# Tree attention: a pair's matmuls grouped by array form, GpSimd's queue written out, V copied by fours

## The chip, the core and the metric

The kernel runs on one core of a Trainium2 chip. The core has a matmul engine (PE, TensorE), whose weights are loaded by separate instructions (PEld); VectorE (DVE); ScalarE (ACT); GpSimd (POOL), which also issues most of the DMAs here; and SyncE (SP), which only issues DMAs. PE writes to PSUM, from which DVE and ACT read; the other tiles are in SBUF. The metric is the device time of one execution in microseconds (us), lower is better.

## The reference

Q, K and V are 8 x 12 x 512 x 64 in fp32: 96 heads of 512 positions. Position i may attend to itself and to its ancestors in a binary heap (parent of i is (i-1)//2), and to nothing else.

```python
scores = np.einsum('bhqd,bhkd->bhqk', Q, K) * scale      # scale = 1/sqrt(64)
scores = scores + (1 - mask) * (-1e9)
weights = np.exp(scores - np.max(scores, axis=-1, keepdims=True))
weights = weights / (np.sum(weights, axis=-1, keepdims=True) + 1e-10)
return np.einsum('bhqk,bhkd->bhqd', weights, V).astype(np.float32)
```

## The kernel before

The heads are worked in **pairs** (pair i is heads 2i and 2i+1, 48 pairs), loaded and stored in **groups** of four (group q is pairs 2q and 2q+1, 24 groups), and the values V lie in buffers of eight heads, called **octets** here (octet o is pairs 4o to 4o+3, 12 octets). A query needs few keys: the top levels of the tree, which all share (one tile of 128 keys, "e1"), and a second tile of 128 keys that depends on the query's quarter ("e2").

A pair takes these steps:

- `transpose(i)` (L227): 32 small PE transposes bring K and Q into the order of the tree, in PSUM (`kqp`); `evac(i)` (L253) copies them to SBUF (`kq`) on DVE.
- `scores1(i)` (L264, L269) and `scores2(i)` (L286, L295): PE writes the mask as a product of codes and adds K·Q; ACT takes the exponential of each (L275, L300) into `e1` and `e2`.
- `values(i, a)` for each head a of the pair (L316, L321, L327): e1 and e2 times V, into `ob`. V has a column of ones, so the sum of the weights comes out beside the values.
- `norm(i)` (L339, L340): DVE takes the reciprocal of that sum and multiplies, into `of`. When both pairs of a group are done, `store` (L348) writes 512 KB.

The tiles that are handed from PE to ACT and DVE (`s1`, `s2`, `kqp`, `ob`) have one buffer each, two PSUM banks of the eight: the values of pair i cannot begin before `norm(i-1)` has read `ob`, and so on.

V comes in by position and must be brought into the order of the tree before it is used as the right operand `vt` (three buffers, one octet each). That is done by copies between partitions: `spread_top` (L193, four copies on POOL for an octet), `spread_l7` (L213, four copies on DVE) and `spread_leaves` (L201, two on DVE). Some copies have a half form of four heads (`h0`, `h1`).

PE uses the array in three forms in this kernel. In the page's rows they are 128\*64 (transposes and the 64-column products of L327), 64\*128 (the scores) and 128\*128 (L316, L321).

The order on every engine is the order of the program text (`manual_schedule`). POOL's queue holds loads, V copies and stores in one line, and an instruction that waits holds back all behind it. So does DVE's queue. Before the main loop, groups 0 to 3 are loaded, pairs 0 and 1 transposed, and octet 0 of V copied by fours. In iteration i: `scores1(i)`, `values(i-1, 0)`, `scores2(i)`, `values(i-1, 1)`, `norm(i-1)`, `transpose(i+2)`, `evac(i+2)`, then V copies of octet i//4+1, then a group of loads (six groups ahead) and, at odd i, a store (six groups back).

Of the kernel before, what the change touches and what calls it, by code (L numbers as in the profile page):

```python
# [26 lines left out]
SELF = (2, 3, 2, 3)  # L27
# [69 lines left out]
def kernel(  # L97
# [54 lines left out]
    NV = 3  # L152
# [11 lines left out]
    qsts, ksts, vsts = {}, {}, {}  # L164
    qTs, kTs, kqps, obs, ets, ofs = {}, {}, {}, {}, {}, {}

    def load_one(name, kept, src, q, parts=1):
        st = loads.tile([P, 4, 4, D], bf16, name=name)
        n = 4 // parts
        for j in range(parts):  # L170
            nc.gpsimd.dma_start(  # L171
                out=st[:, n * j:n * j + n, :, :].rearrange("p h t d -> p h (t d)"),
                in_=src[:, 4 * q + n * j:4 * q + n * j + n, :],
            )
        kept[q] = st

    def load_v(q):
        o, half = divmod(q, 2)
        if half == 0:
            vsts[o] = vloads.tile([P, 8, 4, D], bf16, name="vst")  # L180
        nc.gpsimd.dma_start(  # L181
            out=vsts[o][:, 4 * half:4 * half + 4, :, :].rearrange("p h t d -> p h (t d)"),
            in_=Vr[:, 4 * q:4 * q + 4, :],
        )

    def load(q, parts=1):
        load_one("kst", ksts, Kr, q, parts)
        load_one("qst", qsts, Qr, q, parts)
        load_v(q)

    def spread_top(o, h0=0, h1=8):
        for j in range(4):
            nc.gpsimd.tensor_copy(  # L193
                out=vts[o % NV][32 * j:32 * j + 32, h0:h1, 0, 0:D],
                in_=vsts[o][0:32, h0:h1, UNITS[TOP + j][1], :],
            )

    def spread_leaves(o, r, h0=0, h1=8):

        p = 64 if r else 0  # L200
        nc.vector.tensor_copy(  # L201
            out=vts[o % NV][p:p + 64, h0:h1, 1 + r:4 + r:2, 0:D],
            in_=vsts[o][64:128, h0:h1, r:3 + r:2, :],
        )

    def spread_l7(o, quad, h0=0, h1=8):

        first, slot, step = ((2, 0, 3), (2, 2, -1), (1, 3, -3), (1, 1, 1))[quad]
        src = vsts[o][32:64, h0:h1, slot, :]
        src = bass.AP(  # L210
            src.tensor, src.offset, [list(src.ap[0]), list(src.ap[1]), [step * D, 2], [1, D]]
        )
        nc.vector.tensor_copy(  # L213
            out=vts[o % NV][32 * quad:32 * quad + 32, h0:h1, first:first + 3:2, 0:D], in_=src
        )
# [27 lines left out]

    def evac(i):
        kq = work.tile([P, 2, 16, 32], bf16, name="kq")
        kTs[i] = kq[:, 0, :, :]
        qTs[i] = kq[:, 1, :, :].rearrange("p (t u) c -> p t (u c)", t=4)
        src = kqps[i][:, :, 0:18, :]
        src = bass.AP(
            src.tensor, src.offset,  # L250
            [list(src.ap[0]), [1024, 2], [32, 8], [9 * 32, 2], [1, 32]],
        )
        nc.vector.tensor_copy(  # L253
            out=kq[:, :, :, :].rearrange("p k (x y) c -> p k x y c", y=2), in_=src
        )
# [47 lines left out]
            func=AF.Exp, scale=scale,  # L303
        )

    def values(i, a):
        hh = 2 * (i % 4) + a
        if a == 0:
            obs[i] = psO.tile([P, 2, 512], fp32, name="ob")
        ob, e1, e2, vt = obs[i], ets[i], e2s[i % NE], vts[(i // 4) % NV]  # L310

        def o(t, lo=0, hi=128):
            return ob[lo:hi, a, 65 * t:65 * t + 65]

        for t in range(4):
            nc.tensor.matmul(  # L316
                out=o(t), lhsT=e1[:, a, t, :], rhs=vt[:, hh, 0, 0:D + 1],
                start=t == 0, stop=False,
            )
        for t in (2, 3):  # L320
            nc.tensor.matmul(  # L321
                out=o(t), lhsT=e2[:, a, t, :], rhs=vt[:, hh, 1 + t, 0:D + 1],
                start=False, stop=False,
            )
        for t in (0, 1):
            for lo, tile2 in ((0, SELF[t]), (64, t)):
                nc.tensor.matmul(  # L327
                    out=o(t, lo, lo + 64), lhsT=e2[:, a, t, lo:lo + 64],
                    rhs=vt[:, hh, 1 + tile2, 0:D + 1],
                    start=False, stop=t == 1,  # L330
                )

    def norm(i):
        q, r = divmod(i, 2)
# [15 lines left out]
            in_=ofs[q][:, h0:h0 + n, :, :].rearrange("p h t d -> p h (t d)"),  # L350
        )

    AHEAD = 6
    BEHIND = 6

    load(0, 2)
    load(1)
    spread_top(0, 0, 4)
    load(2)
    spread_top(0, 4, 8)  # L360
    load(3)
    for i in range(2):
        transpose(i)
        evac(i)
    for h in (0, 4):
        for r in range(2):
            spread_leaves(0, r, h, h + 4)
        for j in range(4):
            spread_l7(0, j, h, h + 4)

    loaded, stored = 4, 0
    for i in range(NP + 1):
        q, r = divmod(i, 2)
        if i < NP:
            scores1(i)
        if 1 <= i <= NP:
            values(i - 1, 0)
        if i < NP:
            scores2(i)
        if 1 <= i <= NP:  # L380
            values(i - 1, 1)
            norm(i - 1)
        if i + 2 < NP:
            transpose(i + 2)
            evac(i + 2)
        o = i // 4 + 1
        if o < NQ // 2:
            if i % 4 == 0:
                spread_top(o)
            if i % 4 < 2:  # L390
                spread_l7(o, 2 * (i % 4))
                spread_l7(o, 2 * (i % 4) + 1)
            else:
                spread_leaves(o, i % 4 - 2)
        if loaded < min(NQ, q + 1 + AHEAD):
            load(loaded)
            loaded += 1
        behind = BEHIND if loaded < NQ else 0
        if stored < NQ - 1 and 2 * (stored + behind) + 3 <= i and (r == 1 or loaded == NQ):
            store(nc.gpsimd, stored)  # L400
            stored += 1
        if i == NP - 1:
            store(nc.sync, NQ - 1, 0, 2)
    assert loaded == NQ and stored == NQ - 1
    store(nc.sync, NQ - 1, 2, 1)
    store(nc.scalar, NQ - 1, 3, 1)

# [29 lines left out]
```

## Time and profile before

| | |
|---|---|
| median of 11 runs | 160.11 us (159.2 to 161.58) |
| the profiled execution | 160.66 us, of it span 158.8 us |
| PE busy | 124.5 us (78%) |
| DVE busy | 113.2 us (71%) |
| POOL busy | 104.4 us (66%) |
| ACT busy | 89.0 us (56%) |
| data moved by DMA | 32.30 MB, counted at the destination |

The span is the time from the first to the last instruction on the core; the execution's time is 1.86 us longer. Loads read fp32 from HBM and write bf16 to SBUF (256 KB for a group's K, Q or V), so that the DMA bytes of a load are half of what is read. Engine shares are averages: the first 40 us look different from the rest.

### The profile page before, as it was taken

Reading aid. Unit: us, or ns where it says so; the run is one execution under the profiler, and the core shown is the slowest. Engines: PE = TensorE matmul, PEld = TensorE weight load, DVE = VectorE, ACT = ScalarE, POOL = GpSimd, SP = SyncE. Lnnn points to the kernel's source line nnn. Section 1 sums busy time; section 2 is a strip of 40 time slices with the busy share of each in tenths; the row PEclk is TensorE's granted clock in tenths of the full one; section 3 lists DMA queues with packets and bytes.
Section 4 is the critical chain, followed back from the end, with each engine's and each line's share of the span. In section 5 each row is a group of like instructions: output and inputs, shape, how many; then the busy total and the mean of one; then the engine's idle time right before and its main releaser. Section 6 shows DMA issues by size and latency. Waiting matters only on the chain.

```text
span 158.8 us, 5887 instructions
## 1 busy us (share of the span) xinstructions
PE 124.5 (78%) x2592; PEld 81.3 (51%) x2592; DVE 113.2 (71%) x229; ACT 89.0 (56%) x98; POOL 104.4 (66%) x153
## 2 busy tenths in 40 slices
PE   0386202997499999899999898999999989799860
PEld 0253101674365656575656665666667556565540
DVE  1066307653969989979889889798898997887521
ACT  3025200476156767666776767667768666577730
POOL 7848507993979799987968849769769780111010
PEclk9999855599879999999999999999999999999995
DMA  5999990899999999999999999999999999512342
GB/s 137 158 164 162 171 119 1 110 187 196 196 197 196 197 197 196 197 251 222 258 266 251 223 258 265 253 221 256 268 241 235 376 397 371 203 46 90 136 168 98
DMA packets 42090, 32.30 MB, mean 203 GB/s; under 512 B 1616, under 2 KB 38992, under 8 KB 42064
## 3 DMA queue, kind: packets, MB, share of 16 engines
q0 software_dynamic: 41360, 30.94, 109.4%
q1 hardware_dynamic: 560, 0.85, 1.6%
q8 instruction: 20, 0.33, 0.8%
q10 hardware_dynamic: 144, 0.13, 0.3%
q14 instruction: 6, 0.05, 0.1%
HBM read 38.21 MB, written 12.58 MB: 320 GB/s over the span
## 4 chain that ended last, share of the span: by engine, by line
PE 49%; DVE 21%; DMA 14%; POOL 9%; issue 4%; POOLq 0%; DVEq 0%
DMA vst<-in_V_dram 14%; PE ob L316 11%; PE ob L327 8%; DVE of L340 8%; PE kqp L227 8%; DVE vt L213 7%; PE s L286 6%; PE s L264 5%; PE s L295 4%; PE s L269 4%; DVE kq L253 3%; POOL kst L171 3%; POOL vt L193 3%; POOL qst L171 3%; PE ob L321 3%
## 5 line engine op out<-in xcount | busy, mean ns | idle before, releaser
L275 ACT ACTIVATE e<-s 128x1024 bf16<-128x1024 f32 x48 | 49.1, 1023 | 45.1 <-PE s L269 45.1
L300 ACT ACTIVATE e<-s 128x768 bf16<-128x768 f32 x48 | 38.9, 810 | 18.1 <-PE s L295 16.4
L316 PE MATMUL ob<-vt,e 128*128 128x65 bf16 x384 | 28.8, 198 | 18.7 <-DVE of L340 16.3
L193 POOL COPY vt<-vst 32x512 bf16<-32x512 bf16 (+1 forms) x52 | 32.0, 616 | 17.3 <-DMA vst<-in_V_dram 13.8
L316 PEld LDWEIGHTS <-e 128*128 128x128 bf16 x384 | 17.4, 99 | 44.6 <-DVE of L340 31.8
L253 DVE COPY kq<-kqp 128x1024 bf16<-128x1024 bf16 x48 | 32.7, 681 | 7.6 <-PE kqp L227 7.6
L213 DVE COPY vt<-vst 32x1024 bf16<-32x1024 bf16 (+1 forms) x52 | 27.2, 523 | 10.9 <-DMA vst<-in_V_dram 9.9
L340 DVE TENSOR_TENSOR of<-ob,rec 128x512 f32<-128x512 f32 x48 | 33.2, 691 | 1.7
L348 POOL DMA_DIRECT2D out_dram<-of x23 | 17.7, 769 | 22.8 <-DVE of L340 18.4
L227 PE MATMUL kqp<-ctile,kst 128*64 128x128 bf16 x384 | 20.1, 229 | 8.8 <-DMA kst<-in_K_dram 5.1
L327 PE MATMUL ob<-vt,e 128*64 128x65 bf16 x384 | 24.6, 209 | 0.0
L339 DVE RECIPROCAL rec<-ob 128x8 f32<-128x8 f32 x48 | 10.0, 208 | 19.0 <-PE ob L327 18.2
L321 PE MATMUL ob<-vt,e 128*128 128x65 bf16 x192 | 21.9, 196 | 0.0
L227 PE MATMUL kqp<-ctile,qst 128*64 128x128 bf16 x384 | 20.0, 227 | 2.3 <-DMA qst<-in_Q_dram 2.2
L171 POOL DMA_DIRECT2D qst<-in_Q_dram x25 | 19.1, 763 | 3.4 <-PE s L269 2.2
L171 POOL DMA_DIRECT2D kst<-in_K_dram x25 | 19.2, 766 | 2.1 <-POOLq L421 0.8
L181 POOL DMA_DIRECT2D vst<-in_V_dram x24 | 18.4, 768 | 1.8 <-DMA vst<-in_V_dram 1.3
L264 PE MATMUL s<-ctile 64*128 64x512 bf16 x96 | 19.4, 400 | 0.0
L269 PE MATMUL s<-kq 64*128 64x512 bf16 x96 | 19.0, 392 | 0.0
L295 PEld LDWEIGHTS <-kq 64*128 64x128 bf16 x576 | 16.7, 96 | 4.0 <-issue 1.1
L227 PEld LDWEIGHTS <-kst 128*64 128x64 bf16 x384 | 13.5, 116 | 9.3 <-DMA kst<-in_K_dram 5.4
L295 PE MATMUL s<-kq 64*128 64x64 bf16 (+2 forms) x576 | 18.0, 192 | 0.2 <-issue 0.2
(17 smaller groups left out, 87.0 us busy)
## 6 DMA issues: line engine op xcount, KB each, us to landing
out_dram<-of POOLq DMA_DIRECT2D x23, 512.0 KB, 9.5
vst<-in_V_dram POOLq DMA_DIRECT2D x24, 256.0 KB, 9.3
kst<-in_K_dram POOLq DMA_DIRECT2D x23, 256.0 KB, 8.3
qst<-in_Q_dram POOLq DMA_DIRECT2D x23, 256.0 KB, 8.9
ctile<-tree_consts SPq DMA_DIRECT2D x1, 448.0 KB, 2.9
kst<-in_K_dram POOLq DMA_DIRECT2D x2, 128.0 KB, 3.8
qst<-in_Q_dram POOLq DMA_DIRECT2D x2, 128.0 KB, 4.4
out_dram<-of SPq DMA_DIRECT2D x1, 256.0 KB, 2.2
```

Source lines behind the costliest of these rows:

```text
L171: nc.gpsimd.dma_start(out=st[:, n * j:n * j + n, :, :].rearrange("p h t d -> p h (t d)"), in_=src[:, 4 * q + n * j:4 * q + n * j + n, :],)
L193: nc.gpsimd.tensor_copy(out=vts[o % NV][32 * j:32 * j + 32, h0:h1, 0, 0:D], in_=vsts[o][0:32, h0:h1, UNITS[TOP + j][1], :],)
L213: nc.vector.tensor_copy(out=vts[o % NV][32 * quad:32 * quad + 32, h0:h1, first:first + 3:2, 0:D], in_=src)
L227: nc.tensor.transpose(out=dst, in_=st[i // 2][:, 2 * (i % 2) + a, t, :], identity=perm)
L253: nc.vector.tensor_copy(out=kq[:, :, :, :].rearrange("p k (x y) c -> p k x y c", y=2), in_=src)
L264: nc.tensor.matmul(out=sp[:, a, :], lhsT=k1code[64 * a:64 * a + 64, :], rhs=q1code[64 * a:64 * a + 64, :], start=True, stop=False,)
L275: nc.scalar.activation(out=et[:, :, :, :].rearrange("p a t c -> p (a t c)"), in_=sp[:, :, :].rearrange("p a c -> p (a c)"), func=AF.Exp, s ...
L295: nc.tensor.matmul(out=sp[:, a, t, lo:hi], lhsT=keys(i, a, TILE2[tile2]), rhs=qTs[i][64 * a:64 * a + 64, t, lo:hi], start=False, stop=(t, ...
L300: nc.scalar.activation(out=e2s[i % NE][:, :, :, 32:128].rearrange("p a t c -> p (a t) c"), in_=sp[:, :, :, 32:128].rearrange("p a t c -> p ...
L316: nc.tensor.matmul(out=o(t), lhsT=e1[:, a, t, :], rhs=vt[:, hh, 0, 0:D + 1], start=t == 0, stop=False,)
L327: nc.tensor.matmul(out=o(t, lo, lo + 64), lhsT=e2[:, a, t, lo:lo + 64], rhs=vt[:, hh, 1 + tile2, 0:D + 1], start=False, stop=t == 1,)
L340: nc.vector.tensor_tensor(out=ofs[q][:, 2 * r:2 * r + 2, :, :], in0=o4[:, :, :, 0:D], in1=rec[:, :, :, :].to_broadcast([P, 2, 4, D]), op=A ...
```

## The change

Five things change; the arithmetic, the tiles and their shapes stay, but for the number of `of` buffers.

1. **PE.** In iteration i the order is now `scores1(i)`, `scores2(i)`, then all values of pair i-1: for both heads the 128-column products, then for both heads the 64-column products (`values(i)`, one call for the pair).
2. **POOL's queue** is a generator, `pool_program`, that is advanced step by step. Group 0 comes in as K, Q of two heads, V, K, Q of the other two. From group 2 on, K and Q of group q are issued ahead of the top copies, and V behind them; the top copies belong to group q-2 (first four octets, half an octet at a time) or to octet (q-3)//2 (later).
3. **Stores** go out 12 groups behind the loads, in place of 6; `of` has 15 buffers for 9.
4. **V by fours.** For the first four octets (`FOURS = 4`) the copies on POOL and DVE are made for four heads at a time; before, octet 0 alone.
5. **DVE's V copies** stand elsewhere: half octet f (heads 4f to 4f+3, pairs 2f and 2f+1) in iterations 2f-1 and 2f, three copies in each; later octets o in iterations 4o-3, 4o-2, 4o-1, two copies in each, none in 4o. Before, octet o had two copies in each of 4o-4 and 4o-3 and one in each of 4o-2 and 4o-1.

```diff
-    opool = ctx.enter_context(tc.tile_pool(name="opool", bufs=9))
+    opool = ctx.enter_context(tc.tile_pool(name="opool", bufs=15))
...
+    def values(i):
+
+        obs[i] = ob = psO.tile([P, 2, 512], fp32, name="ob")
+        e1, e2, vt = ets[i], e2s[i % NE], vts[(i // 4) % NV]
...
+        for a in range(2):
+            for t in range(4):
+                product(e1, a, t, 0, start=t == 0, stop=False)
+            for t in (2, 3):
+                product(e2, a, t, 1 + t, start=False, stop=False)
+        for a in range(2):
+            for t in (0, 1):
+                product(e2, a, t, 1 + SELF[t], 0, 64, start=False, stop=t == 1)
+                product(e2, a, t, 1 + t, 64, 128, start=False, stop=t == 1)
...
+    def pool_program():
+
+        load_qk(0, 2)
+        load_qk(1, 1)
+        load_v(1)
+        yield
+        for q in range(2, NQ):
+            load_qk(q, 1)
+            if q < 2 * FOURS + 2:
+                o, half = divmod(q - 2, 2)
+                spread_top(o, 4 * half, 4 * half + 4)
+            elif q % 2 == 1:
+                spread_top((q - 3) // 2)
+            load_v(q)
+            yield
+            if q >= BEHIND:
+                store(nc.gpsimd, q - BEHIND)
+        spread_top(NQ // 2 - 1)
+        for q in range(NQ - BEHIND, NQ - 1):
+            yield
+            store(nc.gpsimd, q)
+
+    def spread_vector(i):
+
+        for f in range(2 * FOURS):
+            o, h = divmod(f, 2)
+            if f == 0 and i == 0:
+                parts = range(6)
+            elif f > 0 and i in (2 * f - 1, 2 * f):
+                parts = range(3) if i == 2 * f - 1 else range(3, 6)
+            else:
+                continue
+            for part in parts:
+                spread_part(o, part, 4 * h, 4 * h + 4)
+        o, step = divmod(i + 3, 4)
+        if FOURS <= o < NQ // 2 and step < 3:
+            spread_part(o, 2 * step, 0, 8)
+            spread_part(o, 2 * step + 1, 0, 8)
...
     for i in range(NP + 1):
         q, r = divmod(i, 2)
         if i < NP:
             scores1(i)
-        if 1 <= i <= NP:
-            values(i - 1, 0)
-        if i < NP:
             scores2(i)
-        if 1 <= i <= NP:
-            values(i - 1, 1)
+        if i >= 1:
+            values(i - 1)
             norm(i - 1)
-        if i + 2 < NP:
-            transpose(i + 2)
-            evac(i + 2)
+        for n in ([1, 2] if i == 0 else [i + 2]):
+            if n < NP:
+                transpose(n)
+                evac(n)
+        spread_vector(i)
```

Three places of the engines' queues, before and after. The rows give the line, the operation, and the tile written and read; `vt_98` is the V buffer of octet 0, `vt_100` that of octet 1.

POOL at the start, before, from the first V copy on:

```order
L193 COPY vt_98<-vst 32x4x64 x4
L171 DMA kst<-in_K_dram 128x4x256
L171 DMA qst<-in_Q_dram 128x4x256
L181 DMA vst<-in_V_dram 128x4x256
L193 COPY vt_98<-vst 32x4x64 x4
L171 DMA kst<-in_K_dram 128x4x256
L171 DMA qst<-in_Q_dram 128x4x256
L181 DMA vst<-in_V_dram 128x4x256
L193 COPY vt_100<-vst 32x8x64 x4
```

The last row copies all of octet 1 and needs V of groups 2 and 3, and the load of group 3 is the row just ahead of it. After, from the first V copy on:

```order
L197 COPY vt_98<-vst 32x4x64 x4
L171 DMA vst<-in_V_dram 128x4x256
L188 DMA kst<-in_K_dram 128x4x256
L188 DMA qst<-in_Q_dram 128x4x256
L197 COPY vt_98<-vst 32x4x64 x4
L171 DMA vst<-in_V_dram 128x4x256
L188 DMA kst<-in_K_dram 128x4x256
L188 DMA qst<-in_Q_dram 128x4x256
L197 COPY vt_100<-vst 32x4x64 x4
```

The last row now copies half of octet 1 and needs V of group 2, behind which K, Q and V of group 3 and K and Q of group 4 have been issued.

DVE at the start, before, from octet 0's copies to the first `norm`:

```order
L201 COPY vt_98<-vst 64x4x2x64 x2
L213 COPY vt_98<-vst 32x4x2x64 x4
L201 COPY vt_98<-vst 64x4x2x64 x2
L213 COPY vt_98<-vst 32x4x2x64 x4
L253 COPY kq<-kqp 128x1024
L213 COPY vt_100<-vst 32x8x2x64 x2
L339 RECIPROCAL rec<-ob 128x8
L340 TENSOR_TENSOR of<-ob,rec 128x512
```

The copies of octet 1 (`vt_100`) stand ahead of the first `norm`. After, from octet 0's first copies to the third `norm`:

```order
L217 COPY vt_98<-vst 32x4x2x64 x4
L205 COPY vt_98<-vst 64x4x2x64 x2
L339 RECIPROCAL rec<-ob 128x8
L340 TENSOR_TENSOR of<-ob,rec 128x512
L257 COPY kq<-kqp 128x1024
L217 COPY vt_98<-vst 32x4x2x64 x3
L339 RECIPROCAL rec<-ob 128x8
L340 TENSOR_TENSOR of<-ob,rec 128x512
L257 COPY kq<-kqp 128x1024
L217 COPY vt_98<-vst 32x4x2x64
L205 COPY vt_98<-vst 64x4x2x64 x2
L339 RECIPROCAL rec<-ob 128x8
```

The first `norm` stands behind half of octet 0 only. The other half is split in two; the last three of its copies stand right ahead of the third `norm`, which is that of pair 2, the first pair that uses them.

PE in one iteration, matmuls only and one of each run, before:

```order
L269 MATMUL s_825<-kq 128x512
...
L316 MATMUL ob<-vt_102,e_752 128x65
...
L327 MATMUL ob<-vt_102,e_2_96 64x65
...
L286 MATMUL s_843<-ctile 128x4x96
...
L295 MATMUL s_843<-kq 128x96
...
L316 MATMUL ob<-vt_102,e_752 128x65
```

The scores of a pair are split by the values of its first head. After:

```order
L273 MATMUL s_826<-kq 128x512
...
L290 MATMUL s_833<-ctile 128x4x96
...
L299 MATMUL s_833<-kq 128x96
...
L316 MATMUL ob<-vt_102,e_762 128x65
...
L316 MATMUL ob<-vt_102,e_2_96 64x65
```

All scores come first, then the values of both heads, the 64-column ones last and next to the transposes, which have the same form.

More of the change, by code (lines that the diff above doesn't have):

```diff
@@ L165 @@
     qTs, kTs, kqps, obs, ets, ofs = {}, {}, {}, {}, {}, {}
[L167 to L175, printed above, removed]
     def load_v(q):
@@ L184, in load_v, with load, load_qk @@
         )
-    def load(q, parts=1):
-        load_one("kst", ksts, Kr, q, parts)
-        load_one("qst", qsts, Qr, q, parts)
+    def load(q):
+        load_qk(q, 1)
         load_v(q)
+    def load_qk(q, parts):
+        pairs = []
+        for name, kept, src in (("kst", ksts, Kr), ("qst", qsts, Qr)):
+            kept[q] = loads.tile([P, 4, 4, D], bf16, name=name)
+            pairs.append((kept[q], src))
+        n = 4 // parts
+        for j in range(parts):
+            for st, src in pairs:
+                nc.gpsimd.dma_start(
+                    out=st[:, n * j:n * j + n, :, :].rearrange("p h t d -> p h (t d)"),
+                    in_=src[:, 4 * q + n * j:4 * q + n * j + n, :],
+                )
+            if j == 0 and parts > 1:
+                load_v(q)
     def spread_top(o, h0=0, h1=8):
```

83 lines of the change are left out of this document (27 added, 56 removed).

## The prediction

> **What bounds the kernel now.** I read first the slices of the page: 40 of 3.97 us each, busy tenths of PE and of the DMA engines, and what the DMAs moved.
>
> ```profile
> span 158.8 us, 5887 instructions
> PE   0386202997499999899999898999999989799860
> DMA  5999990899999999999999999999999999512342
> GB/s 137 158 164 162 171 119 1 110 187 196 196 197 196 197 197 196 197 251 222 258 266 251 223 258 265 253 221 256 268 241 235 376 397 371 203 46 90 136 168 98
> ```
>
> There are two stages. From slice 8 on PE is busy nearly throughout. Ahead of that PE has two holes, and in slices 5 to 7 the DMAs move almost nothing, though most data is still to come. The timeline of POOL and DVE shows why (start, duration, engine, line, in brackets the idle time before and what ended it).
>
> ```profile
> 17.47 0.76 POOL L181 DMA_DIRECT2D vst<-in_V_dram  x1
> 24.62 2.94 POOL L193 COPY vt<-vst 32x512 bf16<-32x512 bf16 x4 [6.38 <-DMA vst<-in_V_dram]
> ...
> 24.59 1.16 DVE L213 COPY vt<-vst 32x1024 bf16<-32x1024 bf16 x2 [7.42 <-DMA vst<-in_V_dram]
> 25.78 0.21 DVE L339 RECIPROCAL rec<-ob 128x8 f32<-128x8 f32 x1
> ```
>
> POOL issues V of group 3 and then waits for that very load, so no further load is queued and the DMAs run dry. DVE waits in the same place, with the first `norm` queued behind. The view of the tile `ob` gives the first and the last reciprocal, my clock for the whole run:
>
> ```profile
> L339 DVE RECIPROCAL rec<-ob x48: 206/208/209, 25.8 to 154.6; 128x8 f32<-128x8 f32 x48
> ```
>
> So 25.8 us until pair 0 is normed, 128.8 us for 47 pairs (2.74 each), and 4.2 us from the last reciprocal to the end. The later stage, by windows (PE, PEld, DVE, ACT, POOL busy with their instructions, clock, DMA share, GB/s; the earlier window is used further down):
>
> ```profile
> 24.00:32.00 8.00, 5.23 (x76) 3.37 (x78) 5.69 (x11) 1.83 (x2) 7.21 (x10) 0.50 0.49 61
> 56.00:128.00 72.00, 67.85 (x1494) 44.73 (x1494) 62.74 (x125) 50.51 (x56) 58.79 (x84) 1.00 1.35 249
> ```
>
> ACT has two instructions a pair, so 72 us hold 28 pairs: 2.57 us each. One such pair in the timeline, PE and DVE:
>
> ```profile
> 139.67 0.39 PE L227 MATMUL kqp<-ctile,kst 128*64 128x128 bf16 x8
> 139.89 0.39 PE L227 MATMUL kqp<-ctile,qst 128*64 128x128 bf16 x8
> 140.21 0.39 PE L264 MATMUL s<-ctile 64*128 64x512 bf16 x2
> 140.44 0.38 PE L269 MATMUL s<-kq 64*128 64x512 bf16 x2
> 140.87 0.30 PE L316 MATMUL ob<-vt,e 128*128 128x65 bf16 x4
> 141.00 0.22 PE L321 MATMUL ob<-vt,e 128*128 128x65 bf16 x2
> 141.15 0.25 PE L327 MATMUL ob<-vt,e 128*64 128x65 bf16 x4
> 141.34 0.34 PE L286 MATMUL s<-ctile 64*128 64x384 bf16 x2
> 141.51 0.36 PE L295 MATMUL s<-kq 64*128 64x96 bf16 x12
> 141.80 0.29 PE L316 MATMUL ob<-vt,e 128*128 128x65 bf16 x4
> 141.93 0.23 PE L321 MATMUL ob<-vt,e 128*128 128x65 bf16 x2
> 142.09 0.25 PE L327 MATMUL ob<-vt,e 128*64 128x65 bf16 x4
> 142.18 0.33 PE L227 MATMUL kqp<-ctile,kst 128*64 128x128 bf16 x6
> ...
> 139.87 0.21 DVE L339 RECIPROCAL rec<-ob 128x8 f32<-128x8 f32 x1 [0.37 <-PE ob L327]
> 140.12 0.69 DVE L340 TENSOR_TENSOR of<-ob,rec 128x512 f32<-128x512 f32 x1
> 140.72 0.68 DVE L253 COPY kq<-kqp 128x1024 bf16<-128x1024 bf16 x1
> 141.44 0.64 DVE L201 COPY vt<-vst 64x1024 bf16<-64x1024 bf16 x1
> 142.38 0.21 DVE L339 RECIPROCAL rec<-ob 128x8 f32<-128x8 f32 x1 [0.30 <-PE ob L327]
> ```
>
> From start to start PE takes 142.18 - 139.67 = 2.51 us a pair. DVE takes 0.25 + 0.60 + 0.72 = 1.57 us for reciprocal, multiply and `kq`, and then V copies. The two engines are close to each other, and `ob` ties them.
>
> **The change: PE's order.** The four L327 products take 142.18 - 142.09 = 0.09 us ahead of transposes, which have the same form, but 141.34 - 141.15 = 0.19 ahead of scores. Two L321 products take 0.15 ahead of L327, where four L316 take 0.13, so by the same-form rate 0.06. The L269 matmuls take 0.43 ahead of values, the like pair L264 ahead of them 0.23. The new order drops one of each: 0.10 + 0.09 + 0.20 = 0.39, so PE's loop becomes 2.12 us. Between zero and that: of the 0.20, part may be a wait for `norm`, whose multiply ends at 140.81, 0.06 before L316. Values from their start to the reciprocal take 142.38 - 141.80 = 0.58 now and, with the first head's 0.13 + 0.06 + 0.09 added, 0.86. From reciprocal over multiply to values and the next reciprocal is then 140.87 - 139.87 + 0.86 = 1.86 us. Both loops fall below what DVE needs when it has copies, so DVE is the bound, and PE's gain is spent there.
>
> **V copies on DVE.** The groups by form give their means.
>
> ```profile
> L213 DVE COPY vt<-vst 32x1024 bf16<-32x1024 bf16 x44 | 24.2, 550 | 10.8 <-DMA vst<-in_V_dram 9.9
> L201 DVE COPY vt<-vst 64x1024 bf16<-64x1024 bf16 x22 | 11.6, 525 | 0.7
> ```
>
> With 0.03 us between instructions (the 0.25 and 0.72 above against 0.21 and 0.68 less rounding) two L213 take 1.16 and two L201 1.11. A later octet has then intervals from reciprocal to reciprocal of 1.57 + 1.16 = 2.73, 2.73, 2.68, and in the iteration without copies 1.86, because DVE is late by then and only the loop through `ob` binds: 10.0 us, or 2.50 a pair against 2.57.
>
> The half copies and the first operands at the start:
>
> ```profile
> 10.47 0.84 DVE L201 COPY vt<-vst 64x512 bf16<-64x512 bf16 x2
> 11.32 1.41 DVE L213 COPY vt<-vst 32x512 bf16<-32x512 bf16 x4
> ...
> 14.10 0.69 DVE L201 COPY vt<-vst 64x512 bf16<-64x512 bf16 x2 [1.36 <-DMA vst<-in_V_dram]
> 14.81 1.64 DVE L213 COPY vt<-vst 32x512 bf16<-32x512 bf16 x4
> ...
> 12.78 0.41 PE L227 MATMUL kqp<-ctile,qst 128*64 128x128 bf16 x8 [0.76 <-DMA qst<-in_Q_dram]
> ```
>
> Six half copies take 2.26 and 2.35 us, so three take 1.15. An octet by fours costs 4.6 us of DVE against 3.4. The interval with three half copies is 1.57 + 1.15 = 2.72. In every second iteration it is longer: the last three copies of half octet f stand right ahead of the `norm` of the pair that needs them, with nothing between. Values of pair 2f wait for these copies, and DVE waits for the values. Only the first head's four e1 products and two or so more can run before; the rest of the 0.86, about 0.70 plus 0.06 to pass on, DVE is idle. So 2.72 and 3.47 alternate in iterations 1 to 12. In 13 and 14 octet 4's copies come on top, which fill that gap: 1.57 + 1.15 + 1.16 = 3.88 each.
>
> **POOL and the stores.** POOL's V copies now wait for a load that has five more queued behind it; at the 196 GB/s of the slices (256 KB in 1.33 us) that is 6.7 us of work, against copies of 2 us, so the DMAs no longer run dry. If a copy were late by more than that, the old stall returns. Q of group 1 is the seventh DMA now as before, so it lands at 12.78 again; from there 0.41 transpose, 0.05 and 0.68 `kq`, 2.3 for six half copies and 0.76 to the first reciprocal: 17.0 us, 8.8 less than now. Stores further back leave the loads alone at the start; POOL issues as many, and the last one still waits for the last pairs. I cost that at nothing; its cover is the lead of the loads (first rival).
>
> **The sum.** Iterations 1 to 12: 6 x (2.72 + 3.47) = 37.1. Two at 3.88: 7.8. Iterations 15 and 16: 2.68 + 1.86 = 4.5. Seven octets at 10.0: 70.0. Three without copies, bound by PE: 3 x 2.12 = 6.4. Together 125.8 against 128.8. Start 17.0, end 4.2: span 147.0, 11.8 less. The profiled execution was 160.66 us, 1.86 over its span, and 0.55 over the median of 160.11; the new time is 148.9 by the one and 148.3 by the other. I say **148.5 us**, a gain of which three quarters come from the start.
>
> **Rivals.**
> First, the loads come late. V of the last group is needed after reciprocal 40, at 17.0 + 37.1 + 7.8 + 4.5 + 60 = 126.4 us. Ahead of it go 9.4 MB of loads alone and 15.3 MB of loads and stores mixed. At the 165 GB/s of the early slices and the 249 of the window, that is 2.5 + 57 + 61 = 121 us. It decides from a mixed rate of 229 GB/s; at 210 it costs 6 us: 154.5. For: slices of 222 and 221. Against: most are above 250. Chance 0.06.
>
> Second, no steady gain: the pairs stay at 2.57, since DVE and PE collide on `ob` as before. 33 intervals at 2.57 are 84.8 in place of 80.9: 152.4. For: DVE already has 62.74 of 72 us. Against: PE has 67.85. Chance 0.14.
>
> Third, slower than before: PE drops to half clock and stays there. After the holes at the start the window from 24 to 32 has clock 0.50, and eight transposes take 0.62 us there against 0.39:
>
> ```profile
> 28.79 0.62 PE L227 MATMUL kqp<-ctile,kst 128*64 128x128 bf16 x8
> ```
>
> PE's loop would be 2.12 x 0.62 / 0.39 = 3.4 us, 0.7 over the mean interval of 2.68. From 17 pairs on that eats the 11.8 us, for all 47 it gives 181 us. For: PE now idles a fifth of each pair, more in the first twelve. Against: the window from 56 to 128 has gaps too and a clock of 1.00, and gaps of 0.75 us are short against the holes of 8. Chance 0.04.
>
> Fourth, DVE's copies get longer, as POOL works more densely beside them. The view of L213 gives 282 ns at the least, 839 at most:
>
> ```profile
> L213 DVE COPY vt<-vst x52: 282/442/839, 11.3 to 139.1; 32x1024 bf16<-32x1024 bf16 x44, 32x512 bf16<-32x512 bf16 x8
> ```
>
> At 0.87 each, an octet's six take 5.2 in place of 3.4, over eight octets 14 us: 162.5. Against: POOL's copies are as many elements as before, so the same number of meetings is likelier. Chance 0.04. The Trainium skill (SBUF — State Buffer, "SBUF: two separate sides") speaks against the change here: it has VectorE and GpSimd share one port pair as an exclusive lock, where the loser waits for the other's whole instruction. The spread of 282 to 839 fits it; by that rule more, shorter copies on both engines meet more often but wait less each time, and the sum would lie between mine and this rival's.
>
> **How the numbers follow.** The forecast has 0.72; its own range is 142 (copies at the median of 442 ns take 4 to 5 us off, shorter half copies 1 to 2) to 152 (a start at 19, copies a tenth longer). The rest has 0.28, of it 0.20 up to 154.5 us. The range 142 to 155 leaves out some 2 in 10. A measurement here can tell 0.5%, about 0.8 us. Slower takes the third rival and half of the fourth, 0.06; same 0.03; faster 0.91.
>
> **What would show it.** Right: first reciprocal near 17 us, no hole in the DMA slices before 60 us, reciprocals 2.7 and 3.5 apart in turn up to pair 14, then 10 us an octet, DVE the busiest engine, PE's loop near 2.1 us where DVE has no copies. Wrong: a DMA wait of DVE or PE after 20 us, a clock of 0.50 past 25 us, or alternate intervals that are equal.

## The result and the profile after

| | before | after |
|---|---|---|
| median | 160.51 us (47 runs, 157.72 to 162.02) | 153.59 us (12 runs, 152.22 to 156.09) |
| ratio, 95% interval | | 0.9627 [0.9592, 0.9661] |
| the profiled execution, of it span | 160.66, 158.8 us | 152.28, 150.4 us |

The change is faster by 3.7%, about half of the 7.3% that was forecast. The ratio takes only the executions within 1.5% of the fastest of each kernel (geometric means 159.26 and 153.32 us); the profiled execution of before lies 1.4 us above this mean and that of after 1.0 below, so some 2.4 of the 8.4 us between the two spans are spread from execution to execution. The slices of the page after (3.76 us each), and a queue of kind "instruction" that the experiments come back to:

```profile
span 150.4 us, 5911 instructions
...
PE   0477797595774959399868878879779696898950
...
DMA  4999999999999999999999999999999439995443
GB/s 134 160 181 194 197 196 195 189 194 197 197 196 199 188 174 256 236 234 270 256 215 267 264 232 242 269 247 227 268 255 239 122 111 300 333 339 192 144 166 115
...
q8 instruction: 20, 0.33, 0.8%
```

The hole in the DMA slices before 40 us is gone, as forecast. PE's row is new: no long zeros at the start, but also no row of nines later. POOL's queue at the place of the old hole waits 1.33 us for V where it waited 6.38, with the next loads behind:

```profile
18.78 1.69 POOL L197 COPY vt<-vst 32x256 bf16<-32x256 bf16 x4 [1.33 <-DMA vst<-in_V_dram]
20.43 0.75 POOL L171 DMA_DIRECT2D vst<-in_V_dram  x1
21.16 0.75 POOL L188 DMA_DIRECT2D kst<-in_K_dram  x1
```

The reciprocals of the 48 norms (tile `ob`), and the later stage by windows (columns as in the prediction):

```profile
L339 DVE RECIPROCAL rec<-ob x48: 206/208/209, 17.1 to 146.2; 128x8 f32<-128x8 f32 x48
```

```profile
56.00:128.00 72.00, 58.95 (x1473) 43.53 (x1474) 64.12 (x129) 46.77 (x54) 53.75 (x76) 1.00 1.23 237
```

The first reciprocal comes at 17.1 us, 8.7 earlier, yet the last one, at 146.2, is only 8.4 earlier: 47 pairs take as long as before, 129.2 against 128.8 us. DVE is now the busiest engine, 64.12 of 72 us against PE's 58.95. The sum of the intervals from reciprocal to reciprocal, by stage (worked out from the 48 starts in the timeline of DVE of each kernel), tells where pairs gained and lost:

| us | first | 1–14 | 15–16 | 17–44 | 45–47 | last to end | span |
|---|---|---|---|---|---|---|---|
| before | 25.8 | 42.7 | 5.1 | 73.9 | 7.1 | 4.2 | 158.8 |
| forecast | 17.0 | 44.9 | 4.5 | 70.0 | 6.4 | 4.2 | 147.0 |
| after | 17.1 | 47.1 | 4.7 | 71.4 | 6.0 | 4.2 | 150.4 |

The start gave what was forecast. The first 14 pairs lost 4.4 us where 2.2 were forecast, and the later ones gained 4.1 where 5.2 were (4.5 + 70.0 + 6.4 against 5.1 + 73.9 + 7.1). In the first 14, DVE's timeline shows a pair of intervals, and PE's the wait in them:

```profile
30.62 0.21 DVE L339 RECIPROCAL rec<-ob 128x8 f32<-128x8 f32 x1 [0.72 <-PE ob L316]
...
31.47 0.68 DVE L257 COPY kq<-kqp 128x1024 bf16<-128x1024 bf16 x1
32.18 0.98 DVE L217 COPY vt<-vst 32x512 bf16<-32x512 bf16 x3
33.20 0.21 DVE L339 RECIPROCAL rec<-ob 128x8 f32<-128x8 f32 x1
...
34.74 0.53 DVE L217 COPY vt<-vst 32x512 bf16<-32x512 bf16 x1
35.28 0.89 DVE L205 COPY vt<-vst 64x512 bf16<-64x512 bf16 x2
36.88 0.21 DVE L339 RECIPROCAL rec<-ob 128x8 f32<-128x8 f32 x1 [0.71 <-PE ob L316]
```

```profile
35.77 0.19 PE L316 MATMUL ob<-vt,e 128*128 128x65 bf16 x1 [1.21 <-DVE vt L205]
36.22 0.62 PE L316 MATMUL ob<-vt,e 128*128 128x65 bf16 x15 [0.26 <-DVE vt L205]
...
81.88 0.30 PE L231 MATMUL kqp<-ctile,kst 128*64 128x128 bf16 x3 [0.40 <-issue]
...
88.62 0.32 PE L299 MATMUL s<-kq 64*128 64x32 bf16 x9 [0.82 <-issue]
...
94.64 0.47 PE L316 MATMUL ob<-vt,e 128*128 128x65 bf16 x10 [0.92 <-issue]
...
100.57 0.36 PE L231 MATMUL kqp<-ctile,qst 128*64 128x128 bf16 x6 [0.64 <-issue]
```

From 30.62 the intervals are 2.58 and 3.68: three copies, then three that the next values wait for (0.71 us of DVE's time lost). The last four rows are of the later stage and were in no step of the prediction: PE stands still, in the middle of a group of matmuls, and waits for nothing that the profile shows ("issue"). After has 8 such holes with a sum of 6.05 us; before had 2 with 0.95 (counted from the rows of PE's timeline).

### The profile page after: what moved, and what is told of

Read it like the earlier page. It is cut to its first block, busy times and chain, and to the rows that moved or that the text cites. A ratio compares the mean times of both kernels' runs of the same rounds, so it can differ in the third digit from the quotient of the medians.

```text
span 150.4 us, 5911 instructions
## 1 busy us (share of the span) xinstructions
PE 112.3 (75%) x2592; PEld 81.4 (54%) x2592; DVE 117.1 (78%) x247; ACT 84.6 (56%) x98; POOL 105.8 (70%) x165
## 4 chain that ended last, share of the span: by engine, by line
DVE 45%; PE 21%; DMA 15%; POOL 8%; issue 7%; ACT 1%; POOLq 0%; ACTq 0%; DVEq 0%
DVE vt L217 13%; DVE of L340 13%; PE ob L316 12%; DMA vst<-in_V_dram 11%; DVE kq L257 9%; DVE vt L205 6%; DVE rec L339 4%; DMA qst<-in_Q_dram 4%; PE kqp L231 4%; POOL vt L197 4%; POOL kst L188 2%; PE s L268 2%; PE s L273 1%; PE s L290 1%; PE s L299 1%
## 5 line engine op out<-in xcount | busy, mean ns | idle before, releaser
L316 PE MATMUL ob<-vt,e 128*128 128x65 bf16 (+1 forms) x960 | 41.6, 199 | 21.8 <-DVE of L340 9.8
L316 PEld LDWEIGHTS <-e 128*128 128x128 bf16 (+1 forms) x960 | 32.1, 104 | 29.9 <-issue 15.1
L197 POOL COPY vt<-vst 32x256 bf16<-32x256 bf16 (+1 forms) x64 | 33.3, 520 | 16.1 <-PE kqp L231 7.2
L217 DVE COPY vt<-vst 32x512 bf16<-32x512 bf16 (+1 forms) x64 | 29.3, 458 | 1.3
L231 PE MATMUL kqp<-ctile,qst 128*64 128x128 bf16 x384 | 20.6, 231 | 2.6 <-issue 1.9
L299 PEld LDWEIGHTS <-kq 64*128 64x128 bf16 x576 | 17.0, 96 | 9.3 <-issue 3.4
L188 POOL DMA_DIRECT2D qst<-in_Q_dram x25 | 19.6, 783 | 2.9 <-PE s L299 1.2
L299 PE MATMUL s<-kq 64*128 64x64 bf16 (+2 forms) x576 | 18.3, 191 | 1.4 <-issue 1.4
L290 PE MATMUL s<-ctile 64*128 64x384 bf16 x96 | 16.6, 339 | 0.8 <-issue 0.6
L231 PEld LDWEIGHTS <-qst 128*64 128x64 bf16 x384 | 14.6, 117 | 2.1 <-DMA qst<-in_Q_dram 1.2
```

The costliest lines, as they stand in the source:

```text
L188: nc.gpsimd.dma_start(out=st[:, n * j:n * j + n, :, :].rearrange("p h t d -> p h (t d)"), in_=src[:, 4 * q + n * j:4 * q + n * j + n, :],)
L197: nc.gpsimd.tensor_copy(out=vts[o % NV][32 * j:32 * j + 32, h0:h1, 0, 0:D], in_=vsts[o][0:32, h0:h1, UNITS[TOP + j][1], :],)
L217: nc.vector.tensor_copy(out=vts[o % NV][32 * quad:32 * quad + 32, h0:h1, first:first + 3:2, 0:D], in_=src)
L231: nc.tensor.transpose(out=dst, in_=st[i // 2][:, 2 * (i % 2) + a, t, :], identity=perm)
L299: nc.tensor.matmul(out=sp[:, a, t, lo:hi], lhsT=keys(i, a, TILE2[tile2]), rhs=qTs[i][64 * a:64 * a + 64, t, lo:hi], start=False, stop=(t, ...
L316: nc.tensor.matmul(out=ob[lo:hi, a, 65 * t:65 * t + 65], lhsT=e[:, a, t, lo:hi], rhs=vt[:, 2 * (i % 4) + a, tile_v, 0:D + 1], **flags,)
```

## The experiments

Each kernel was timed beside executions of the kernel before on the same chip; ratios are to those. The stages (first reciprocal, sums of intervals, span, number and sum of PE's holes, in us) are those of one profiled execution each, and executions of one kernel spread by 1 to 4 us, so small differences between stages mean little. The first reciprocal alone lies between 17.1 and 18.1 us in the six profiled kernels that start alike (after, e3 to e7). The theory on the first 14 pairs: they are dear because their copies stand right ahead of the norm. On the later ones, from e5 on: PE's holes are its instructions that come in late. The rivals are in the expectations.

| kernel | median us | ratio, 95% interval | first | 1–14 | 17–44 | span | PE's holes |
|---|---|---|---|---|---|---|---|
| after | 153.59 | 0.9627 [0.9592, 0.9661] | 17.1 | 47.1 | 71.4 | 150.4 | 8, 6.05 us |
| e1_pe_only | 154.94 | 0.9671 [0.9593, 0.9749] | 25.1 | 40.6 | 72.3 | 153.1 | 15, 12.05 |
| e2_no_group | 167.08 | 1.0404 [1.0277, 1.0531] | 18.9 | 51.7 | 75.9 | 164.4 | 0 |
| e3_half_early | 151.06 | 0.9455 [0.9360, 0.9549] | 18.0 | 44.6 | 71.7 | 149.4 | 9, 6.58 |
| e4_fours2 | 151.91 | 0.9521 [0.9409, 0.9632] | 18.1 | 41.6 | 73.1 | 149.7 | 9, 8.72 |
| e5_thin_stores | 151.05 | 0.9389 [0.9326, 0.9452] | 17.5 | 46.6 | 69.5 | 148.5 | 2, 0.68 |
| e6_behind6 | 153.89 | 0.9515 [0.9432, 0.9597] | 17.9 | 46.2 | 73.5 | 152.5 | 8, 8.12 |
| e7_early_fours2 | 151.16 | 0.9396 [0.9330, 0.9461] | 17.9 | 41.8 | 73.3 | 149.5 | 13, 10.18 |
| e8_act_leaves | 147.25 | 0.9098 [0.9016, 0.9180] | 16.8 | 36.9 | 71.1 | 143.5 | 10, 8.22 |
| e9_warm | 154.17 | 0.9495 [0.9449, 0.9541] | – | – | – | – | – |
| e10_act_warm | 147.72 | 0.9220 [0.9168, 0.9271] | 17.3 | 37.6 | 71.2 | 145.9 | 12, 10.07 |
| e11_act_thin | 141.50 | 0.8835 [0.8783, 0.8886] | 17.5 | 38.3 | 68.7 | 139.8 | 6, 4.70 |
| e12_act_behind6 | 145.94 | 0.9032 [0.8953, 0.9111] | 16.6 | 38.8 | 73.8 | 144.5 | 7, 4.18 |

**e1_pe_only**: PE's order alone, in the kernel before (with `values` as in the change).

```diff
...
-        if 1 <= i <= NP:
-            values(i - 1, 0)
         if i < NP:
             scores2(i)
-        if 1 <= i <= NP:
-            values(i - 1, 1)
+        if i >= 1:
+            values(i - 1)
```

> The kernel before with PE's new order alone (all scores, then the values of both heads, 64-column products last). Theory (DVE is the bound once PE's loop is at 2.1 us): the late pairs go from 2.57 to about 2.5 us and the start stays, so 157 to 158 us against 160.5. Rival (PE is the bound): 0.39 us for each of 47 pairs, 142 us.

```profile
L335 DVE RECIPROCAL rec<-ob x48: 183/207/209, 25.1 to 149.0; 128x8 f32<-128x8 f32 x48
```

Measured 154.94 us: better than the theory, where DVE takes the gain, and far from the rival. The first reciprocal stays near the old place, at 25.1. Of the 5.7 us of span that go, 2.1 are in intervals 1 to 14, 0.2 in 15 and 16, 1.6 in 17 to 44, 1.1 in the last three and 0.6 at the start. Interval 4 takes 8.13 us, as DVE waits for V once more, as it also does in before:

```profile
39.07 1.59 DVE L213 COPY vt<-vst 32x1024 bf16<-32x1024 bf16 x2 [4.98 <-DMA vst<-in_V_dram]
```

So one part of the five, with the old start, gives 3.3% of the 3.7% that all five give.

**e2_no_group**: the kernel after with PE's old order (and the old `values`, by heads).

```diff
...
+        if i >= 1:
+            values(i - 1, 0)
+        if i < NP:
             scores2(i)
         if i >= 1:
-            values(i - 1)
+            values(i - 1, 1)
             norm(i - 1)
```

> The changed kernel with PE's old order, all else as changed. Theory: the start keeps its 8.7 us, the late pairs, 82.1 us for 33 intervals, go back to PE's loop of 2.51 us and more where DVE has two copies in an iteration, so 156 to 158 us against 153.6. Rival (PE's order is worth nothing here because DVE binds anyway): 153 to 154 us.

Measured 167.08 us, slower than before, which neither expected. One pair of the first 14 in the timeline (PE, then ACT and DVE):

```profile
25.35 0.19 PE L325 MATMUL ob<-vt,e 128*128 128x65 bf16 x1 [1.17 <-DVE vt L205]
25.98 0.19 PE L325 MATMUL ob<-vt,e 128*128 128x65 bf16 x1 [0.44 <-DVE vt L205]
...
26.36 0.50 PE L290 MATMUL s<-ctile 64*128 64x384 bf16 x2
...
27.28 0.81 ACT L304 ACTIVATE e<-s 128x768 bf16<-128x768 f32 x1 [2.39 <-PE s L299]
...
27.91 0.21 DVE L343 RECIPROCAL rec<-ob 128x8 f32<-128x8 f32 x1 [1.99 <-PE ob L331]
```

PE waits 1.17 us for the copies with the first head's products, and the scores behind them wait along. ACT then waits 2.39 us for the scores and DVE 1.99 for the second head. This pair is the longest of the 14, with the clock at half from 26.05 us on; in the like places later, at full clock, DVE waits 1.40 us, where it lost 0.72 after. The parts are not a sum: with the old order the rest of the change costs 4.0%, with the new order it brings 0.4% more than the order alone (0.9627 against 0.9671, intervals that overlap). The rows fit this reading: late copies cost less in after because what waits for them stands last in PE's row.

**e3_half_early**: all six half copies one iteration earlier.

```diff
-            elif f > 0 and i in (2 * f - 1, 2 * f):
-                parts = range(3) if i == 2 * f - 1 else range(3, 6)
+            elif f > 0 and i == 2 * f - 1:
+                parts = range(6)
```

> The changed kernel with all six half copies of half octet f in iteration 2f-1 and none in 2f, so that no copy stands right ahead of the norm that waits for it. Theory (the alternate wait is what the first pairs lose by): 6 waits of 0.7 to 0.75 us go and the intervals without copies fall to 1.9, so 4 to 5 us less: 149 us. Rival (the first pairs are slow by the half clock and by longer copies): no change, 153 to 154 us.

```profile
30.27 0.21 DVE L339 RECIPROCAL rec<-ob 128x8 f32<-128x8 f32 x1 [0.36 <-PE ob L316]
...
31.83 1.66 DVE L217 COPY vt<-vst 32x512 bf16<-32x512 bf16 x4
33.51 0.69 DVE L205 COPY vt<-vst 64x512 bf16<-64x512 bf16 x2
34.23 0.21 DVE L339 RECIPROCAL rec<-ob 128x8 f32<-128x8 f32 x1
...
36.12 0.21 DVE L339 RECIPROCAL rec<-ob 128x8 f32<-128x8 f32 x1 [0.36 <-PE ob L316]
```

Intervals of 3.96 and 1.89, 5.85 a pair of them, where after has 6.26 at this place. Intervals 1 to 12 take 35.8 against 39.9 us, the 4 to 5 us of the theory. Of that only some is seen at the end: interval 13 becomes 5.99 us, as copies of half octet 7 and of octet 4 now meet there, with PE at half clock for 3.2 us of it, and the first reciprocal is 1.0 later, which the edit does not touch. 151.06 us, ratio 0.9455, its interval clear of after's.

**e4_fours2**: half copies only for the first two octets (`FOURS = 2`).

> The changed kernel with V by fours for two octets in place of four. Theory (half copies and the waits behind them cost more than they give): two octets save 1.2 us of DVE work each and four waits of 0.75 us, 148 to 149 us. Rival (copies of a whole octet need V that lands later and stall DVE and POOL): 154 us or more, with DVE waiting for V near 30 us.

The first 14 intervals fall by 5.5 us, and 15 to 16 (6.1 against 4.7) and 17 to 44 (73.1 against 71.4) give 3.1 back, the last three 0.6, the start 1.0. DVE does not wait for V, as the rival has it: after 20 us it has no wait for a DMA. 151.91 us, an interval that overlaps after's.

**e7_early_fours2**: both edits.

> Both at once: all six half copies in iteration 2f-1, and by fours for two octets only. If the two gains of 2.5 and 1.7 us add up: 149.5 us. If both remove the same waits: 151 to 152 us.

151.16 us: the same first 14 as e4 alone (41.8), later pairs as there (73.3). The two remedies are for the same loss, and don't add up.

**e5_thin_stores**: is the hole of PE tied to the DMAs? POOL's stores write one head in four; three quarters of the output of those groups are left out.

```diff
-                store(nc.gpsimd, q - BEHIND)
+                store(nc.gpsimd, q - BEHIND, 0, 1)
...
-            store(nc.gpsimd, q)
+            store(nc.gpsimd, q, 0, 1)
```

> The changed kernel, with each of GpSimd's 23 stores cut to one head of four: three quarters of the output of those groups is left out. It asks what PE's holes without a releaser are, 0.4 to 1.2 us each, which come 128 matmuls apart in the late pairs of the changed kernel and hardly before. Theory (PE's instructions come in blocks by DMA, late where the other DMAs are dense): with 8.7 MB less to move the holes shrink below 0.3 us, and the time falls by 2 to 3 us, 151 us. Rival (a block takes as long in either case, and shows wherever PE has no work queued): holes as before, time within 1 us of 153.6.

The hole that stood at 100.57 in after, now:

```profile
100.34 0.36 PE L231 MATMUL kqp<-ctile,qst 128*64 128x128 bf16 x6 [0.31 <-issue]
```

Two holes are left, 0.31 and 0.37 us long, and 17 to 44 take 69.5, below the forecast 70.0. Holes at the same matmul of the same pair, shorter with fewer bytes on the DMA queues, say that PE waited for something that DMAs bring. Its distance says what: a pair has 54 matmuls (16 transposes, not the 32 that the text on the kernel before gives: the page counts 384 for K and 384 for Q of 48 pairs; 18 scores, 20 values). After the hole at 88.62 there are 9 of 12 L299 still to run in that pair, after that at 94.64 10 of 20 L316: 9 + 20 + 16 = 45 to the end of that row of values and transposes, 54, and 18 + 10 = 28, together 127. From there to 100.57 it is 10 + 16, 54, and 18 + 20 + 10, together 128. Queue q8 of the page brought instructions in 20 packets, 0.33 MB, and PE ran 2592 matmuls and as many weight loads: 5184 / 20 = 259 for each packet, and 128 matmuls with their loads are 256. The trace has the time of every DMA packet, and the packets of q8, 16,384 bytes each, can be set beside PE's holes. After:

| us | | | | | | | | |
|---|---|---|---|---|---|---|---|---|
| packet on q8 starts | 79.52 | 86.24 | 92.34 | 98.18 | 104.23 | 110.22 | 116.41 | 134.42 |
| hole of PE ends | 81.88 | 88.62 | 94.64 | 100.57 | 106.49 | 112.65 | 118.85 | 136.60 |
| that is later by | 2.36 | 2.38 | 2.30 | 2.39 | 2.26 | 2.43 | 2.44 | 2.18 |

The same holds for all 101 holes of the table above and of before: each ends 2.2 to 2.6 us after a packet on q8 has started (one 2.9). In e2, which has none, PE comes to each such place 2.3 us or more after the packet's start (places counted in steps of 127.7 matmuls from those of after). So PE waits for a block of its own instructions. The packet for the next block starts late where the DMAs have much to move: between 55 and 120 us on average 3.8 us after PE has come to the block before, in e5 2.7. Together with the 2.4 us that gives 6.2 us for a block, and a block is 2.36 pairs: an estimate of 2.6 us a pair as the least that PE can take there. The runs have about this pace where a hole stands at every block: 2.61 us a pair in after (six blocks from 81.88 to 118.85), 2.60 in e1 (13 blocks from 59.69 to 139.81), 2.64 in e8 (eight blocks from 65.40 to 115.41), 2.63 in e7 and 2.70 in e6. This is why e1's later pairs came nowhere near the 2.12 us of the rival's loop.

**e6_behind6**: stores six groups back (`BEHIND = 6`).

> The changed kernel with stores 6 groups behind the loads again. Theory (stores are covered by the lead of the loads): within 1 us of 153.6. Rival (stores between the first loads hold V copies back): 156 us or more, with waits of DVE for V ahead of 40 us.

153.89 us, with an interval that overlaps after's by a little: the start is 17.9 (17.1), the first 14 46.2 (47.1). Stores six back did not hurt the start, as forecast; 17 to 44 are 2.1 us longer in the profiled execution, which took 154.40 us where that of after took 152.28.

**e8_act_leaves**: from here on, versions to beat both. The two copies of L205 go to ACT, which is 47 of 72 us busy, on top of e3.

```diff
-        nc.vector.tensor_copy(
+        nc.scalar.copy(
             out=vts[o % NV][p:p + 64, h0:h1, 1 + r:4 + r:2, 0:D],
...
-            spread_part(o, 2 * step, 0, 8)
-            spread_part(o, 2 * step + 1, 0, 8)
+            for part in ((0, 1), (2, 4), (3, 5))[step]:
+                spread_part(o, part, 0, 8)
```

> All six half copies in iteration 2f-1, and the leaves' copies (two of six) on ACT in place of DVE; in later octets two copies of DVE in 4o-3, one of DVE and one of ACT after, and so on. Theory (DVE binds): DVE loses some 1.1 us of each octet of 10 us and 0.8 us of each half octet, so 6 to 9 us less than the 151 us with DVE's leaves: 142 to 145 us. Rival (PE's loop, its holes and ACT bind next): 149 us or more.

```profile
56.00:120.00 64.00, 55.06 (x1347) 40.50 (x1345) 48.72 (x99) 54.02 (x62) 46.33 (x67) 0.99 1.29 241
```

147.25 us, between the theory and the rival. The first 14 fall to 36.9, but the 28 later intervals stay at 71.1, though DVE is down to 48.72 of 64 us. PE has 55.06, ACT 54.02, and PE's holes are 8.22 us in ten, nine of them at successive blocks from 65.40 to 115.41 us. Right for the first stage, wrong for the second, where PE keeps the pace of its blocks, 2.64 us a pair.

**e9_warm** and **e10_act_warm**: nine matmuls of 512 columns that lead to nothing, five ahead of the first transpose and two behind each of the next two transposes, to have PE at full clock for the first pairs; in after, and in e8.

> The changed kernel with nine matmuls of 512 columns more, on constants, into a buffer that is overwritten: five ahead of the first transpose, two behind each of the next two. Theory (the first two intervals of 3.6 and 3.7 us are long because PE runs at half clock until 21 us): they fall to 2.8 and 3.5, the first reciprocal stays near 17 us, the time falls by 1 us. Rival (they are long by V's landing or by the copies): no interval changes, the time is the same or up to 1 us longer.

> The same nine matmuls in the kernel that has the leaves' copies on ACT (147.25 us). Theory: 1 us less, 146 us. Rival: the same.

e9's five executions go from 151.59 to 160.27 us, the profiled one is that of 160.27, so its stages are not read, and the ratio rests on two of the five (151.59 and 152.23 us): inconclusive. e10 gains nothing over e8 (0.9220 against 0.9098), as the rival has it: its clock is full from 17.24 us, ahead of its first reciprocal, and its first two intervals are 0.4 us shorter than e8's, but the first reciprocal is 0.4 later. What half clock costs at the start stays open.

**e11_act_thin**: e8 with thin stores, the same part of the output left out as in e5.

> The kernel with the leaves' copies on ACT, with each of GpSimd's stores cut to one head of four (three quarters of the output of those groups is left out). In that kernel the first 14 intervals took 36.9 us, but intervals 17 to 44 took 71.1, as with all copies on DVE. Theory (PE's holes at block boundaries, not an engine, hold the late pairs there): the holes go, the 28 intervals take 63 to 65 us, the time falls to 139 to 141 us. Rival (ACT with 1.83 us and copies, or PE's own loop, binds): 69 us or more, the time above 144.5.

141.50 us. The 28 intervals fall only to 68.7; holes are still 4.70 us. Of the 3.7 us by which its span is below e8's, 2.9 come behind the last reciprocal (4.0 us against 6.9, as fewer bytes are left to store). In the 28 intervals 2.4 us are gained; six blocks still come late, and what else holds these pairs is not shown.

**e12_act_behind6**: e8 with stores six back, so that less is left at the end.

> The kernel with the leaves' copies on ACT (147.25 us), stores 6 groups behind the loads in place of 12. There the last reciprocal is at 136.6 us and the end at 143.5, 6.9 us later, against 4.2 in both kernels before, with the DMAs full to the end. Theory (so many stores wait for the last loads that the last one is late once the pairs are faster): the tail falls to 4.2 to 4.5 us and the time by 2 to 2.5 us, 145 us. Rival (earlier stores hold the late loads and PE's instructions back by as much, as 28 intervals of 73.5 against 71.4 us hinted in the run with copies on DVE): 147 us or more.

Waits of e12 (sum, times, longest):

```profile
PE ob L316 <- DVE of L340: 13.0, 13, 3.8
DVE vt L217 <- DMA vst<-in_V_dram: 8.0, 8, 2.0
```

The end falls to 4.0 us as the theory has it, and the later pairs pay: 73.8, where DVE now waits 8.0 us for V, from 50 us on (in after DVE has no wait for a DMA after 20 us). That V comes in late behind the stores fits, as their place is all that differs from e8. 145.94 us, ratio 0.9032: the fastest whole kernel of these runs, with an interval that overlaps e8's.

## Why the prediction was wrong in size

The forecast was 148.5 us and 153.59 came out: 5.1 us. The span is 3.4 of it (150.4 against 147.0): 2.2 in intervals 1 to 14, 0.2 in 15 and 16, 1.4 in 17 to 44, and −0.4 in the last three. Two steps failed: the first 14 intervals were mis-sized, and the later pairs had no term for PE's instructions. The other 1.7: the text put 1.5 on top of the span, the execution that was profiled has 1.9, and it lies 1.3 under the median of its kernel, where that of before lies 0.15 above.

- **The start: right, its closeness in part luck.** 17.0 forecast, 17.1 measured, and by the chain given: POOL no longer waits for its newest load. But PE begins the transposes of Q of group 1 at 12.14 us where 12.78 was forecast, and transposes, copies and the last step take 0.7 us longer in sum.
- **"2.72 and 3.47 alternate in iterations 1 to 12": a step that failed, by its sizes (2.7 us, of which 13 and 14 give 0.5 back).** The pattern is there, but the intervals with three L217 sum to 17.7 where 16.3 was forecast, the others to 22.2 where 20.8 was. The wait for the copies was priced right: DVE stands 0.72 and 0.71 us in the two places shown, where the text had 0.70, while PE stops 14 times for them:

```profile
PE ob L316 <- DVE vt L205: 9.8, 14, 1.2
```

  One L217 and two L205 took 1.375 us in the mean of six, against 1.15, which is the whole excess of those intervals. What goes with it shows in the timeline: a pair of L205 takes 1.27 us at 47.64, while POOL's own copies run, and 0.61 where they don't:

```profile
47.40 2.02 POOL L197 COPY vt<-vst 32x512 bf16<-32x512 bf16 x3
47.64 1.27 DVE L205 COPY vt<-vst 64x512 bf16<-64x512 bf16 x2
...
62.54 0.61 DVE L205 COPY vt<-vst 64x512 bf16<-64x512 bf16 x2
```

  The Trainium skill (SBUF — State Buffer, "SBUF: two separate sides") has VectorE, in its two-port modes, and GpSimd take a shared port pair in turns, whole instructions at a time. The durations agree with it: of the 16 half copies of L205 the eight that overlap a copy of POOL take 539 ns on average, the eight others 332. No run here removed POOL's copies to show it.
  In the intervals with three L217 the excess is mostly at half clock: the first is 3.60 where 2.72 was forecast, with PE at half clock until 21 us (rows of 0.62 us for eight transposes) and without a pause from 17.8 us on, which the text had seen in before and left out of this sum; and interval 11 is 3.08, with half clock until 51.9 us.
- **"DVE is the bound", "seven octets at 10.0": 71.4 in place of 70.0, the other step that failed.** Copies were no longer than forecast:

```profile
L217 DVE COPY vt<-vst 32x1024 bf16<-32x1024 bf16 x32 | 17.1, 535 | 0.7
L217 DVE COPY vt<-vst 32x512 bf16<-32x512 bf16 x32 | 12.2, 381 | 0.6
...
L205 DVE COPY vt<-vst 64x1024 bf16<-64x1024 bf16 x16 | 7.7, 481 | 0.4
L205 DVE COPY vt<-vst 64x512 bf16<-64x512 bf16 x16 | 7.0, 435 | 0.4
```

  Whole copies took 535 and 481 ns against 550 and 525. The sum had no term for PE's own instructions. From 81.88 to 118.85 us they set the pace: 2.61 us a pair where 2.50 was forecast, which over these 14.2 pairs is 1.6 us. With thin stores, where the holes are nearly gone, this stage takes 69.5; and in e8, where DVE is busy for 48.72 of 64 us in place of 64.12 of 72, it stays at 71.1.
- **PE's loop: right.** A pair at the end, where DVE has no copies, from its transposes to its values, after:

```profile
140.00 0.39 PE L231 MATMUL kqp<-ctile,kst 128*64 128x128 bf16 x8
140.23 0.39 PE L231 MATMUL kqp<-ctile,qst 128*64 128x128 bf16 x8
140.55 0.39 PE L268 MATMUL s<-ctile 64*128 64x512 bf16 x2
140.77 0.38 PE L273 MATMUL s<-kq 64*128 64x512 bf16 x2
140.99 0.33 PE L290 MATMUL s<-ctile 64*128 64x384 bf16 x2
141.15 0.36 PE L299 MATMUL s<-kq 64*128 64x96 bf16 x12
141.44 0.79 PE L316 MATMUL ob<-vt,e 128*128 128x65 bf16 x20
```

  From transpose to values 1.44 us; values take 0.62 to the next transposes where nothing waits (83.36 to 83.98). 2.06 us for a loop, forecast 2.12, before 2.51.
- **"A gain of which three quarters come from the start": wrong.** e1 has the old start and gives 3.3% of the 3.7%. The new start brings 8.7 us, and the copies by fours and in their new places take most of it back in the 14 pairs behind it (47.1 us against 40.6 in e1, where they still hold the wait of 5 us for V); e2 shows how much they would take without PE's order.
- **The rivals.** No load came late: DVE and PE have no wait for a DMA after 20 us. The pairs did not stay as they were, but 17 to 44 fell by 2.5 us where 3.9 were forecast, so the second rival has a part, by PE's blocks more than by a collision on `ob`. A clock of 0.50 past 25 us, one of the prediction's signs of being wrong, came at 48.5 us and went after 3.4 us, so the third has a small part. Copies were longer where they met POOL's, though the mean of whole copies was not, so the fourth has its place above all in the first 12 pairs.

**Left open**: the price of half clock at the start; whether POOL's copies cause the longer ones of DVE; and what holds the later pairs with thin stores (69.5 us in e5, 68.7 in e11), where the blocks come late only now and then.

## What to carry to other kernels

Put what an engine produces for an in-order consumer at least one step ahead of it, and put the work that may wait last in the consumer's row: the same late copies cost DVE 0.7 us a time behind the scores and 1.4 us ahead of them. Price a change of order in each stage where it acts, by the intervals of one repeated instruction, and try its parts alone and together, because they need not add (3.3% faster by the order alone, 4.0% slower by the rest alone, 3.7% faster by both). When an engine gets free time in its row, look for what its full queue had covered: here the late arrival of its own instructions, 6.2 us for a block of 128 matmuls while the DMAs were busy.

## What was not expected of the hardware

- PE stands still for 0.4 to 1.2 us about every 128 matmuls, with no semaphore to wait for, when its order lets it run ahead, until 2.2 to 2.6 us after a 16 KB packet of instructions has started; 0.3 to 0.4 with a quarter of the bytes stored, and not at all in e2, where PE comes later than the packets. Fewer holes don't make a faster kernel: e2 has none and is the slowest.
- The clock fell to half in the middle of the run, with PE never still for long. Two windows of 3.40 us of after:

```profile
45.10:48.50 3.40, 1.80 (x39) 1.15 (x34) 3.25 (x9) 2.46 (x4) 1.64 (x3) 1.00 1.47 201
48.50:51.90 3.40, 2.94 (x41) 1.96 (x42) 2.32 (x6) 0.11 (x1) 3.34 (x6) 0.50 1.45 190
```

  In the first PE is busy for 1.80 us, and its longest stop is 1.14 us, a wait for L205; in the second the clock is 0.50. The Trainium skill (TensorE: Matmul & The Clock Gate, Part 1) has the clock halved after an idle window of about 3.4 us. Here the half clock lasted about as long as such a window, but there was no stop of that length ahead of it: a half-busy window was enough. In the 14 profiles the clock falls to 0.50 between 30 and 125 us 23 times, each time right behind a window of 3.41 us in which PE was busy for 1.95 us or less; not every such window is followed by it (e3 at 57.1 us: busy 1.59 us, clock 1.00 after). The prediction's "gaps of 0.75 us are short" was no safe reason, though here it cost little: the intervals of 4.12 and 3.08 us are 0.5 and 0.3 us above the mean of the others of their kind without half clock.
